# Handing out mixer steps by an account of VectorE's pending work in a hybrid retention / gated-DeltaNet step

## The chip, the cores and the metric

The kernel runs on one core of one Trainium2 chip. The metric is the device time of one execution in microseconds; a time of the kernel is the median of several runs.

## The reference

One inference step of a one-layer model with two token streams: 128 context tokens and 256 noisy latent tokens, 384 in all, of width 4096. For both:

```
mod = silu(c) @ w_ada + b_ada                  # shift, scale, gate: 3 x 4096
u   = rms_norm(h) * (1 + scale) + shift
proj = u @ w_in                                # 4096 x 16448
o_ret = retention(q, k, v), both directions    # 8 heads of 256, chunks, decay per head
o_gdn = gated_delta(conv(q), conv(k), conv(v)) # 16 heads of 128, both directions
h = h + gate * (concat(norm(o_ret)*silu(g), norm(o_gdn)*silu(z)) @ w_out)
y = rms_norm(h) * final_norm_w
```

The gated delta rule needs, for each head, direction and chunk, the inverse of a unit lower triangular matrix. The context's final states are outputs, and the latent scans start from cached states. All is float32.

## The kernel before

Every large product is done three times (high*high, high*low, low*high): a weight piece of 128x512 arrives by DMA on SP's queue, ScalarE casts it to the high part `wh` (L210), and VectorE subtracts to get the low part `wl` (L211). This is `split_tile` (L204). Pieces are prepared up to four ahead of the one that TensorE multiplies.

The work on TensorE is one long list of pieces, set when the kernel is built. First come the modulation matrices (tile `ada`) mixed with the first weight rows of many column groups. Then come 32 column groups of `w_in`, four to a pair of gated-delta heads and one retention head: group 4p gives k and q of gated-delta pair p, 4p+1 its v and z, 4p+2 and 4p+3 those of retention head p. Between them lie the pieces of the gate modulation (tile `adg`). Last come eight groups of `w_out`. When a group ends, VectorE and ScalarE take its sums out of PSUM into tiles `rawt` (`sum_done`, L540: an addition where an earlier part of the sum was kept, else copies).

When k and q of a pair or a head are there, a *mixer job* joins the list `bg_list`: `gdn(p)` (L743, 126 steps) or `ret(h)` (L1057, 33 steps). A job is a Python generator that writes a few instructions and yields. What it yields is a number of ns for the step just written, nothing (a step of `SLOT` = 1000), or a negative number: a wait for a DMA (5000 and 8000 in `gdn`). The longest VectorE steps are those of the triangular inverse, rows 2 to 31, each one multiplication (L854) and one reduction (L856), which yield 390 + 2.1 i² for row i. Before the first pair, `gates` (L671, 33 steps) prepares the decays.

The order of all instructions is a sum done at build time, with a clock of its own, here called planner ns. After each triple of large matmuls, `slot(ns)` (L186) adds 480 or 639 to the clock `now` and takes it from `next`; if `next` is at most 0, `bg_step` (L166) writes one step of the oldest job, and what `pace` (L152) returns is added to `next`. `pace` takes a base (1000 for an empty yield, else at least 500 and `PACE` times the ns; a negative yield as it is) and multiplies it by a factor f, held between `FMIN` and `FMAX`:

```
f = (due[end] - now - MARGIN) / rem
```

Here `rem` is the job's `COST` less the bases so far (for a retention head before the last, plus the cost of the next `gdn`), and no step gets less than `FLOOR` = 600. The due times come from the list of pieces: that of `gdn` p is the piece five before the end of group 4(p+1) (L1221), where the `rawt` tiles of pair p are wanted again; those of `gdn` 7 and `ret` 7 are pieces of the first `w_out` group (L1329, L1330).

If a job isn't done by then, it is drained: `new_raw` (L509) and `mix_load` (L1238) call `bg_drain`, which writes all its remaining steps in a row, with no large matmul between them. Every engine works through its instructions in the order written. Near the end, `mix_load` (POOL's queue) brings the mixers' outputs back from DRAM (`d_mix`) through two `mixl` buffers, and `mix_put` (L1246) splits them into `uh` and `ul`, the left factors of the `w_out` groups; this is written five pieces ahead of the piece that needs it.

Of the kernel before, what the change touches and what calls it, by code (L numbers as in the profile page):

```python
# [44 lines left out]
PRE = 5  # L45
RING = 5
RAW_RING = 4
PACE = 1.4
CG = 166e3
CR = 45e3  # L50
COST = {"gates": 35e3, "gdn": CG, "ret": CR}
FMIN = 0.5
FLOOR = 600.0
GATE = 1500
FMAX = 1.0
MARGIN = 1200.0
MIN_SLOT = 500.0
AHEAD = 5
# [8 lines left out]
def hybrid_step(ctx: ExitStack, tc: tile.TileContext, x_prompt, x_sample, state_ret_fwd, state_ret_bwd,  # L67
# [78 lines left out]

    urgent = []

    clock = {"next": 0.0, "now": 0.0}
    left, due = {}, {}  # L150

    def pace(tag, ns):  # L152

        base = -ns if ns and ns < 0 else (SLOT if ns is None else max(MIN_SLOT, PACE * ns))
        if tag[0] not in COST:
            return base
        left[tag] = left.get(tag, COST[tag[0]]) - base
        if ns and ns < 0:
            return base
        kind, p = tag  # L160
        rem, end = max(left[tag], base), tag
        if kind != "gdn" and p < 7:
            rem, end = rem + COST["gdn"], ("gdn", p + 1)
        return max(FLOOR, base * min(FMAX, max(FMIN, (due[end] - clock["now"] - MARGIN) / rem)))

    def bg_step():  # L166


        while urgent:
            try:  # L170
                return pace(("urgent", 0), next(urgent[0]))
            except StopIteration:
                urgent.pop(0)
        while bg_list:
            tag, job = bg_list[0]
            try:
                return pace(tag, next(job))
            except StopIteration:
                bg_list.pop(0)
        return SLOT  # L180

    def bg_drain(tag=None):
        while bg_list and (tag is None or any(t == tag for t, _ in bg_list)):
            bg_step()

    def slot(ns):  # L186
        clock["now"] += ns
        clock["next"] -= ns
        if clock["next"] <= 0:
            clock["next"] = max(clock["next"], -SLOT) + bg_step()  # L190


# [11 lines left out]
    def split_tile(raw, shape, place=None):  # L204
        if place:
            h, lo = place
        else:
            h = wpool.tile(shape, F32R, tag="wh", name="wh", bufs=RING)
            lo = wpool.tile(shape, F32R, tag="wl", name="wl", bufs=RING)
        A.copy(h, raw)  # L210
        V.tensor_tensor(lo, raw, h.bitcast(F32), op=ALU.subtract)  # L211
        return h, lo

    class Gemm:
# [15 lines left out]
        def prepare(self, i):  # L230
            if i % 2 == 0:
                self.raw = load_piece(self.src, self.chunks, self.rows(self.ks[i]), min(2, len(self.ks) - i))
            return split_tile(self.raw[:, i % 2], [128, 2, 256], self.lend and self.lend(i))

        def compute(self, i, hl):
            if self.ps is None:
                if self.ps_alloc:
                    self.ps = [self.ps_alloc(n) for n in range(3)]
                else:
                    if self.kind == "T":  # L240
                        while urgent:
                            bg_step()
                    shape, m = ([128, T], 4) if self.kind == "T" else ([128, 512], 3)
                    self.ps = [ps_main.tile(shape, F32, tag=f"mm{n}", name=f"mm{n}") for n in range(m)]
# [7 lines left out]
            for n, ps in enumerate(self.ps):  # L252
                for m, (h, lo) in self.hold:
                    k = self.ks[m]
                    st, sp = m == 0, m == end
                    if self.kind == "T":
                        wh = h[:, n // 2, (n % 2) * 128:(n % 2) * 128 + 128]
                        wl = lo[:, n // 2, (n % 2) * 128:(n % 2) * 128 + 128]
                        PE.matmul(ps, wh, high(k), start=st, stop=False)  # L259
                        PE.matmul(ps, wh, low(k), start=False, stop=False)  # L260
                        PE.matmul(ps, wl, high(k), start=False, stop=sp)  # L261
                        slot(3 * 160)
                    else:
                        a, b = high(k)[:, n * 128:n * 128 + 128], low(k)[:, n * 128:n * 128 + 128]
                        PE.matmul(ps, a, h, start=st, stop=False)  # L265
                        PE.matmul(ps, a, lo, start=False, stop=False)  # L266
                        PE.matmul(ps, b, h, start=False, stop=sp)  # L267
                        slot(3 * 213)
                if i == end:
                    self.done(n, ps)  # L270
# [4 lines left out]
    class Gates:  # L275
# [9 lines left out]
        def prepare(self, i):  # L285
            raw = load_piece(w_in, [(16384, 64)], i, 8)
            return split_tile(raw[:, :, 0], [128, 8, 64])
# [14 lines left out]
    class Ada:  # L302
# [14 lines left out]
        def compute(self, i, raw):  # L317
            if self.ps is None:
                self.ps = self.ps_alloc()
            cs = slice(256 * (i // NK), 256 * (i // NK) + 256)  # L320
            for q in range(4):
                k = i % NK + q
                PE.matmul(self.ps[32 * q:32 * q + 32, cs], cst[:, 2 * k:2 * k + 32], raw[:, q, 0],  # L323
                          start=(k < 4), stop=(k >= NK - 4), tile_position=(0, 32 * q))
            slot(450)
            if i + 4 == self.width // 256 * NK:
                self.done(self.ps)
            return 1
# [180 lines left out]
    def new_raw(owner):  # L509
        while len(live) >= RAW_LIVE:  # L510
            bg_drain(live[0])
            assert live[0] != owner
            o = live[0]
            while live and live[0] == o:
                live.pop(0)
        live.append(owner)
        return rawp.tile([128, 768], F32, tag="raw", name="rawt", bufs=RAW_LIVE)
# [22 lines left out]
    def sum_done(g, partial, last):  # L540
        kind, own, rt = groups[g][0], owner(g), rts[g // 2]

        def pre():
            if partial != "sbuf":
                kept[g] = [new_raw(own) for _ in range(2)]
            if partial == "dram":
                for i in range(2):
                    G.dma_start(out=kept[g][i], in_=d_part[g][:, 768 * i:768 * i + 768])

        def done(n, ps):  # L550
            box = kept[g]
            if kind == "T":
                t = box[n // 2][:, T * (n % 2):T * (n % 2) + T]
                if partial:
                    V.tensor_tensor(t, ps, t, op=ALU.add)  # L555
                else:
                    A.copy(t, ps)
            else:
                for i in range(2):
                    t = box[i][:, 256 * n:256 * n + 256]  # L560
                    if partial:
                        V.tensor_tensor(t, ps[:, 256 * i:256 * i + 256], t, op=ALU.add)
                    else:
                        (A.copy if i else V.tensor_copy)(t, ps[:, 256 * i:256 * i + 256])  # L564
            if last and n == (3 if kind == "T" else 2):
                for i, nm in enumerate("vz" if g % 2 else ("qk" if own[0] == "ret" else "kq")):
                    rt[nm] = box[i]
                if g % 2 == 0:
                    bg_list.append((own, gdn(own[1], rt) if own[0] == "gdn" else ret(own[1], rt)))
        return pre, done  # L570
# [822 lines left out]
```

## Time and profile before

| | |
|---|---|
| median of 3 runs | 3338.46 us (3335.72 to 3339.66) |
| profiled execution | 3342.99 us, span 3340.9 us |
| PE busy | 3256.4 us, 97% of the span |
| DVE busy | 1840.7 us, 55% |
| ACT busy | 1198.9 us, 36% |
| POOL busy | 292.2 us, 9% |

PE is TensorE, DVE is VectorE, ACT is ScalarE, POOL is GpSimd. PE's busy time counts a matmul from its start to its modelled end, and neighbours overlap, so small losses hide in it: the start-to-start distance of matmuls shows them, the idle column does not wholly. The mixers run from about 800 us to 2815 us of the span. The rows of the profile stand in the prediction.

### The profile page before, as it was taken

How to read it: one execution, taken by the hardware profiler on the slowest of the kernel's cores; microseconds unless marked ns; L12 is line 12 of the kernel's file. 1: busy time of each engine (PE TensorE's matmuls, PEld its weight loads, DVE VectorE, ACT ScalarE, POOL GpSimd, SP SyncE). 2: the span in 40 equal slices, each digit the busy share in tenths (PEclk: the TensorE clock that was granted, in tenths of full speed). 3: DMA queues.
4: the chain of work that ended last, by engine and by line, in shares of the span. 5: the costliest groups of instructions: out<-in, count | busy, mean ns of one | idle time of the engine just before them, and what ended most of it. 6: DMA issues, size and time to landing. Idle time of an engine off the chain costs nothing. (4 is left out here: it accounts for less than half of the span.)

```text
span 3340.9 us, 51824 instructions
## 1 busy us (share of the span) xinstructions
PE 3256.4 (97%) x19312; PEld 2706.2 (81%) x19312; DVE 1840.7 (55%) x3811; ACT 1198.9 (36%) x2588; POOL 292.2 (9%) x463
## 2 busy tenths in 40 slices
PE   5999999999999999999999999999999999999998
PEld 2778888877699779789789779779779877788887
DVE  2554433335855756754856746746844845444444
ACT  3322222224245235244345245235244334333333
POOL 0000000001101001001011001011000012100000
PEclk9999999999999999999999999999999999999999
DMA  9888998975534554544645645554644556645444
GB/s 304 290 287 272 330 311 266 297 251 159 179 105 135 169 153 149 179 145 140 192 146 152 185 129 156 173 154 147 177 153 141 160 153 188 187 145 170 145 151 170
DMA packets 594236, 626.14 MB, mean 187 GB/s; under 512 B 38978, under 2 KB 577042, under 8 KB 593984
## 3 DMA queue, kind: packets, MB, share of 16 engines
q1 hardware_dynamic: 570096, 551.04, 52.7%
q0 software_dynamic: 23888, 71.79, 7.3%
q8 instruction: 151, 2.47, 0.3%
q14 instruction: 101, 0.83, 0.1%
HBM read 590.37 MB, written 32.33 MB: 186 GB/s over the span
## 5 line engine op out<-in xcount | busy, mean ns | idle before, releaser
L211 DVE TENSOR_TENSOR wl<-raw,wh 128x512 fp32r<-128x512 f32 x1274 | 854.3, 687 | 939.8 <-ACT wh L210 935.8
L210 ACT CAST wh<-raw 128x512 fp32r<-128x512 f32 x1274 | 756.6, 620 | 1350.6 <-DMA raw<-in_w_in_dram 659.0
L265 PE MATMUL mm<-wh,uh 128*128 128x512 f32 x1920 | 784.3, 408 | 9.1 <-ACT rawt L564 5.6
L266 PE MATMUL mm<-wl,uh 128*128 128x512 f32 x1920 | 755.3, 393 | 6.4 <-DVE wl L211 5.8
L267 PE MATMUL mm<-wh,ul 128*128 128x512 f32 x1920 | 752.9, 392 | 0.0
L259 PE MATMUL mm<-uh,wh 128*128 128x384 f32 x2048 | 721.0, 352 | 6.2 <-DVE ul L555 3.8
L261 PE MATMUL mm<-uh,wl 128*128 128x384 f32 x2048 | 689.4, 337 | 0.0
L260 PE MATMUL mm<-ul,wh 128*128 128x384 f32 x2048 | 688.8, 336 | 0.0
L265 PEld LDWEIGHTS mm<-wh,uh 128*128 128x128 f32 x1920 | 362.2, 189 | 141.0 <-issue 48.2
L259 PEld LDWEIGHTS mm<-uh,wh 128*128 128x128 f32 x2048 | 387.3, 189 | 51.2 <-issue 34.6
L266 PEld LDWEIGHTS mm<-wl,uh 128*128 128x128 f32 x1920 | 362.7, 189 | 81.2 <-DVE wl L211 14.1
L267 PEld LDWEIGHTS mm<-wh,ul 128*128 128x128 f32 x1920 | 362.2, 189 | 78.2 <-DVE ul L1248 0.7
L260 PEld LDWEIGHTS mm<-ul,wh 128*128 128x128 f32 x2048 | 387.6, 189 | 3.9 <-issue 2.9
L261 PEld LDWEIGHTS mm<-uh,wl 128*128 128x128 f32 x2048 | 386.8, 189 | 0.0
L854 DVE TENSOR_TENSOR tmp<-M 48x4 f32<-48x4 f32 (+14 forms) x240 | 189.3, 789 | 3.4
L323 PE MATMUL ada<-adar,cst 128*32 128x256 f32 x2048 | 147.5, 404 | 26.9 <-DMA adar<-in_w_ada_dram 26.9
L645 DVE SCALAR_TENSOR_TENSOR acc<-rawt,cw,acc 128x126 f32<-128x126 f32 (+3 forms) x384 | 133.8, 413 | 12.8 <-ACT acc L640 12.8
L266 PE MATMUL o<-wl,uh 128*128 128x512 f32 x354 | 138.1, 390 | 0.2 <-DVE wl L211 0.2
L265 PE MATMUL o<-wh,uh 128*128 128x512 f32 x354 | 138.0, 390 | 0.2 <-ACT wh L210 0.2
L267 PE MATMUL o<-wh,ul 128*128 128x512 f32 x354 | 137.9, 390 | 0.0
L323 PEld LDWEIGHTS ada<-adar,cst 128*32 128x32 f32 x2048 | 53.8, 112 | 92.7 <-DMA adar<-in_w_ada_dram 42.8
L856 DVE TENSOR_REDUCE M<-tmp 48x2 f32<-48x4 f32 (+14 forms) x240 | 121.6, 507 | 8.3
(321 smaller groups left out, 2522.7 us busy)
## 6 DMA issues: line engine op xcount, KB each, us to landing
raw<-in_w_in_dram SPq DMA_DIRECT2D x1028, 256.0 KB, 3.6
adar<-in_w_ada_dram SPq DMA_DIRECT2D x256, 512.0 KB, 5.7
raw<-in_w_ada_dram SPq DMA_DIRECT2D x128, 512.0 KB, 4.3
raw<-in_w_out_dram SPq DMA_DIRECT2D x256, 256.0 KB, 3.1
rawt<-d_part POOLq DMA_DIRECT2D x26, 384.0 KB, 4.3
d_part<-spill POOLq DMA_DIRECT2D x9, 768.0 KB, 7.4
gr<-d_gc POOLq DMA_DIRECT2D x16, 384.0 KB, 7.4
d_mix<-rawt POOLq DMA_DIRECT2D x32, 192.0 KB, 2.8
```

The source lines that it names most:

```text
L210: A.copy(h, raw)
L211: V.tensor_tensor(lo, raw, h.bitcast(F32), op=ALU.subtract)
L259: PE.matmul(ps, wh, high(k), start=st, stop=False)
L260: PE.matmul(ps, wh, low(k), start=False, stop=False)
L261: PE.matmul(ps, wl, high(k), start=False, stop=sp)
L265: PE.matmul(ps, a, h, start=st, stop=False)
L266: PE.matmul(ps, a, lo, start=False, stop=False)
L267: PE.matmul(ps, b, h, start=False, stop=sp)
L323: PE.matmul(self.ps[32 * q:32 * q + 32, cs], cst[:, 2 * k:2 * k + 32], raw[:, q, 0], start=(k < 4), stop=(k >= NK - 4), tile_position=(0, ...
L645: V.scalar_tensor_tensor(out=dst[:, lo:hi], in0=x[:, lo + o:hi + o], scalar=w(t), in1=dst[:, lo:hi], op0=ALU.mult, op1=ALU.add)
L854: V.tensor_tensor(t, M[0:48, 0:i, 0:i].rearrange("p j c -> p c j"), M[0:48, i:i + 1, 0:i].to_broadcast([48, i, i]), op=ALU.mult)
L856: V.tensor_reduce(M[0:48, i, 0:i], t, axis=AX.X, op=ALU.add)
```

## The change

The planner keeps a third clock, `dve`: the time at which VectorE will have done what was given to it. Each mixer step, each weight split (`SPLIT` = 690) and each addition out of PSUM (690) is booked on it. `slot` writes no step while the account is `BACKLOG` = 1500 or more ahead of `now`. The base of a step no longer has 40% on top (`PACE` 1.0), the jobs' costs are lower, and f may rise to 2.0, so that steps may be stretched as well as shortened. No instruction is added or removed; the order in which mixer steps stand between the large matmuls changes.

```
-PACE = 1.4
-CG = 166e3
-CR = 45e3
-COST = {"gates": 35e3, "gdn": CG, "ret": CR}
+PACE = 1.0
+CG = 130e3
+CR = 28e3
+SPLIT = 690.0
+STEP = 300.0
+BACKLOG = 1500.0
+COST = {"gates": 26e3, "gdn": CG, "ret": CR}
-FMAX = 1.0
+FMAX = 2.0
...
-    clock = {"next": 0.0, "now": 0.0}
+    clock = {"next": 0.0, "now": 0.0, "dve": 0.0}
+
+    def dve(ns):
+
+        clock["dve"] = max(clock["dve"], clock["now"]) + ns
+
...
         while urgent:
             try:
-                return pace(("urgent", 0), next(urgent[0]))
+                ns = next(urgent[0])
+                dve(STEP)
+                return pace(("urgent", 0), ns)
...
             tag, job = bg_list[0]
             try:
-                return pace(tag, next(job))
+                ns = next(job)
+                dve(STEP if ns is None or ns < 0 else ns)
+                return pace(tag, ns)
...
-        if clock["next"] <= 0:
+        if clock["next"] <= 0 and clock["dve"] - clock["now"] < BACKLOG:
             clock["next"] = max(clock["next"], -SLOT) + bg_step()
...
         V.tensor_tensor(lo, raw, h.bitcast(F32), op=ALU.subtract)
+        dve(SPLIT)
         return h, lo
...
                 if partial:
                     V.tensor_tensor(t, ps, t, op=ALU.add)
+                    dve(SPLIT)
```

## The prediction

> **What bounds the kernel now.** I read the page's busy times first, then the busy times by stage, then whom TensorE waited for.
>
> ```profile
> PE 3256.4 (97%) x19312; PEld 2706.2 (81%) x19312; DVE 1840.7 (55%) x3811; ACT 1198.9 (36%) x2588; POOL 292.2 (9%) x463
> ```
>
> ```profile
> core 0: us, PE busy (x) PEld busy (x) DVE busy (x) ACT busy (x) POOL busy (x), PEclk, DMA share, GB/s
> 800.00:1000.00 200.00, 191.92 (x1172) 158.45 (x1172) 134.36 (x299) 79.43 (x185) 19.85 (x29) 0.99 0.50 150
> 1000.00:2770.00 1770.00, 1762.20 (x10419) 1486.11 (x10418) 1097.17 (x2345) 700.25 (x1595) 203.37 (x304) 1.00 0.52 157
> 2770.00:2870.00 100.00, 95.31 (x416) 76.74 (x415) 52.65 (x99) 45.38 (x92) 24.59 (x44) 0.98 0.59 175
> 2870.00:3341.00 471.00, 458.00 (x2017) 378.45 (x2015) 202.17 (x306) 155.74 (x275) 21.73 (x38) 0.99 0.51 160
> ```
>
> PE bounds it. In the mixer stages PE is idle for 8.1, 7.8 and 4.7 us, and no instruction is taken away, so all that a new order can gain is of the size of these waits. DVE has room on average (1097 of 1770 us), so only its order can hurt. The waits that end PE's idle time:
>
> ```profile
> engine line waited for: us in total, times, longest us
> PE mm L266 <- DVE wl L211: 5.8, 11, 1.8
> PE mm L265 <- ACT rawt L564: 5.6, 4, 2.3
> PE mm L265 <- ACT uh L1247: 2.8, 1, 2.8
> PE bg L1106 <- ACT qkT L1097: 1.9, 1, 1.9
> PE bg L1051 <- ACT o L1046: 1.7, 1, 1.7
> PE mm L259 <- DVE rawt L562: 1.5, 1, 1.5
> PE mm L259 <- DVE rawt L555: 0.9, 2, 0.5
> ```
>
> The first, second, sixth and seventh (13.8 us, 18 times) are large matmuls that wait for a weight split or for PSUM to be emptied. What holds these up:
>
> ```profile
> 1901.66 1.90 DVE L854 TENSOR_TENSOR tmp<-M 48x961 f32<-48x961 f32 x1
> 1903.59 1.15 DVE L856 TENSOR_REDUCE M<-tmp 48x31 f32<-48x961 f32 x1
> 1904.66 1.06 DVE L564 COPY rawt<-mm 128x256 f32<-128x256 f32 x3
> 1902.59 0.39 PE L266 MATMUL mm<-wl,uh 128*128 128x512 f32 x1
> 1905.53 0.50 PE L265 MATMUL mm<-wh,uh 128*128 128x512 f32 x1 [2.32 <-ACT rawt L564]
> ```
>
> The copies out of PSUM stand behind a row step of the triangular inverse that takes 3.05 us. From L266 to the next L265 lie 2.94 us; two matmuls at the usual 0.23 us would be 0.46. The loss is 2.48 us where the idle column has 2.32: each wait costs about 0.2 more than it shows. And it costs clock:
>
> ```profile
> 974.70:978.10 3.40, 1.74 (x10) 1.11 (x9) 0.32 (x2) 1.58 (x6) 1.35 (x1) 1.00 0.52 154
> 978.10:981.50 3.40, 3.40 (x13) 3.31 (x12) 1.58 (x3) 2.60 (x4) 0.60 (x1) 0.51 0.00 0
> 1906.50:1910.00 3.50, 3.50 (x10) 2.69 (x10) 1.90 (x3) 1.19 (x3) 1.97 (x4) 0.51 0.33 89
> 2865.70:2869.10 3.40, 3.40 (x10) 2.63 (x9) 0.83 (x2) 0.54 (x2) 2.86 (x5) 0.50 0.53 78
> 976.97 0.92 PE L1051 MATMUL bg<-ident,o 128*128 128x128 f32 x3 [1.66 <-ACT o L1046]
> 2756.25 0.78 PE L1051 MATMUL bg<-ident,o 128*128 128x128 f32 x3
> ```
>
> After the waits of 1.66, 2.32 and 2.8 us the granted clock (third number from the end) is 0.5 for 3.4 us: half of 3.4, 1.7 us, is lost each time.
>
> **The change part by part.** What moves is only the place of 1,300 steps, so I stepped the planner's sums through the list of pieces, with the old numbers and the new. One planner ns is 1.3 ns on the chip: the head transposes of pairs 0 and 7 stand at 738.5 and 2112.0 thousand planner ns and at 976.97 and 2756.25 us.
>
> Demand on DVE in planner ns: `gdn` books 64.9 thousand in named steps and 49 others at 300, 79.6 in all; its bases sum to 153.1 with `PACE` 1.4 and 128.0 with 1.0 (19.0 of it DMA waits). The weight splits book 690 for each piece of 1920, 36%. Before, a named step got 1.4 times its ns, times f: f was 0.83 for pair 0 (86% of DVE + 36% = 122%), and 1.0 for pairs 1, 2 and 4 to 7 (71 + 36 = 107%). By the new account, kept for the old order, VectorE's backlog passes 5000 in the row steps of most pairs, and has 5585 at the wait of 1902 us shown above. In the new order f is 1.0 to 1.5 in most pairs, 453 slots are held back, and outside the two drains below the backlog passes 5000 in pairs 0 and 3 alone. No emptying of PSUM falls any more beside the steps that wait for the inverse's DMA.
>
> (a) The waits for splits and PSUM: 13.8 + 18 x 0.2 + 1.7 of clock = 19.1 us is all there is. At the group ends from 800 thousand on the account has at most 3.3 thousand instead of 5.6, so I take 17. Bounds: -19.1; and -8, if half of them come back at other places.
>
> (b) The end of the `mixl` loads. PE waits 2.8 us for the last `uh` and then loses 1.7 of clock, since the last load lands late (the chain's row):
>
> ```profile
> 2859.54 4.61 DMA mixl<-d_mix
> ```
>
> The loads go through two buffers at 2.2 us each and PE takes 2.0 a piece, so PE catches up with them. In the new order `gdn` 7 and `ret` 7 run beside these loads and PE waits in (d), so the loads get ahead. Before `uh` of piece 30, PE has five pieces, 10.2 us, after (d); `d_mix`, `mixl` and the split take 0.6 + 2.8 + 3.2 + 1.1 = 7.7:
>
> ```profile
> d_mix<-rawt POOLq DMA_DIRECT2D x32, 192.0 KB, 2.8
> mixl<-d_mix POOLq DMA_DIRECT2D x32, 192.0 KB, 3.2
> ```
>
> I take the whole wait as gone: 2.8 + 0.2 + 1.7, -4.7. The other bound is 0. POOL's queue stands in order: a load written behind `gdn` 7's output DMAs waits for them, but those wait for matmuls that PE reaches at the same place, five pieces ahead of need.
>
> (c) Pair 0 comes too late. `gates` ends at 625.6 thousand (611.3 before), and pair 0 is due at 750.2. In these 124.6 thousand VectorE's account must take 79.6 for the pair and 64 splits, 44.2: 123.8, and 13 thousand of DMA waits let no step through. That doesn't fit: at the due time 21 steps are left, the tail from the first state product on, and `new_raw` writes them in a row. PE then has nothing between them:
>
> ```profile
> 1189.48 2.17 ACT L989 ACTIVATE wk<-bg,br 128x128 f32<-128x128 f32 x8 [5.27 <-PE bg L983]
> 1196.83 1.13 DVE L973 SCALAR_TENSOR_TENSOR wk<-bg,gt_neg,rawt 128x128 f32<-128x128 f32 x4 [0.20 <-PE bg L967]
> 1199.80 1.14 ACT L989 ACTIVATE wk<-bg,br 128x128 f32<-128x128 f32 x4 [3.37 <-PE bg L983]
> 1207.15 1.03 PE L1019 MATMUL bg<-S,rawt 128*128 128x256 f32 x4
> 1208.41 1.38 DVE L1031 SCALAR_TENSOR_TENSOR o<-bg,gt_eg,o 128x128 f32<-128x128 f32 x4
> 1210.78 1.35 POOL L135 TENSOR_TENSOR c<-c,half_c 128x6 f32<-128x6 f32 x1 [13.80 <-DVE c L1040]
> 1212.36 1.87 ACT L1046 ACTIVATE o<-o,c 128x128 f32<-128x128 f32 x6 [1.56 <-DVE c L1042]
> ```
>
> These rows of pair 1 give the chain. The last part is unpadded: from the end of L1019, 1208.2, to the third of six L1046, 1213.3, PE has nothing of this job: 5.1 us, and 0.9 for the second head. Before it stand 1.13 + 2.17 + 1.13 + 1.14 = 5.6 us in which PE waits if the two heads don't overlap at all. They alternate, so I take a fifth, 1.2. Idle: 7.2; bounds 5.1 and 11.6. A stretch of half clock follows, 1.7 (bounds 0 and 3.4). Gone is the wait at 976.97: 1.66 + 0.2 + 1.7 = 3.6. Sum +5.3 (bounds +1.5 and +11.4). Queued behind the drained tail on POOL is the load of `rawt` for the next group; the addition that needs it comes five pieces later, which covers it.
>
> (d) The last head comes too late. `gdn` 7 may now be stretched (f = 1.5) to its own due time: it ends at 2178 (2116 before). `ret` 7 is due at 2185.0 and has bases of 26.9 thousand: 10 of 33 steps fit, and `mix_load` writes 23 in a row.
>
> ```profile
> 2804.76 1.03 PE L1154 MATMUL bg<-rawt,kd 128*128 128x256 f32 x4
> 2799.97 0.58 ACT L1136 COPY o_r<-bg 128x512 f32<-128x512 f32 x1 [3.35 <-PE bg L1130]
> 2803.43 1.00 DVE L1140 SCALAR_TENSOR_TENSOR o_r<-bg,rq_dec,o_r 128x256 f32<-128x256 f32 x2
> 2806.35 0.89 POOL L135 TENSOR_TENSOR ssr<-ssr,half_c 128x3 f32<-128x3 f32 x1
> 2808.51 0.88 DVE L1159 SCALAR_TENSOR_TENSOR o_r<-o_r,ssr,rawt 128x256 f32<-128x256 f32 x2
> ```
>
> After the product with v: 0.58 + 2 x 1.00 + 0.8 for squares and sum + 0.89 + 1.36 = 5.6, beside two L1154 of 1.03: 3.5 us idle, 0.8 for the copies of q and k, and about 2 because the ten steps ahead (8 us of rotary products) fill DVE. Idle 6.3; with 1.7 of clock, and without the 1.9 at L1106: +6 (bounds +1.5 and +11).
>
> (e) Pair 3 is just in time with f at 0.6, as pair 0's tail was before at 0.67. I price its tail at what that one cost, +3.6 (bounds 0 and +5). Pair 5 goes down to 0.7 at its very end only: 0.
>
> (f) Outside the mixers steps move by a slot at most: 0, within 1 either way.
>
> Sum: -17 - 4.7 + 5.3 + 6 + 3.6 = -6.8 us. The profiled execution has 3342.99, 4.5 above the median; with the same step from the median, 3338.46 - 6.8 = 3331.7 us.
>
> A rule on the clock bears on (c) and (d). The rows above show half clock after waits of 1.66 to 2.8 us. The Trainium skill, TensorE: Matmul & The Clock Gate, section "What's actually happening", has the clock fall only after an idle window of about 3.4 us; these three rows speak against so long a wait. By it (d) would keep its clock and come out at +4.3, and the sum at -8.5.
>
> **The rivals.** (1) The drains decide: slower. One mechanism, the steps written in a row at the two due times, at its upper bounds: +11.4 and +11, with pair 3 at +3.6. With (a) at -8 and (b) at 0 that is +18, 3356 us. For it: they are certain in the order, and the 5.1 us gap is unpadded. Against: most of what is drained is PE's own work, and it is due anyway. It decides from drains of about 15 us together beyond what (a) brings back. (2) No change: VectorE's work is the same and a row step still takes 3.05 us, so waits come back before other matmuls; (a) brings 9, and the sum is +1: 3339 us. For it: in 1000 to 2770 us PE lost only 7.8 us in idle time. Against: the account at the group ends falls by 2000 and more. (3) A gap longer than those seen costs two stretches of half clock: (c)'s 5.1 us is such a gap, and with (d)'s, 3.4 more: 3335 us. The same page, section "HAM oscillation", says that a gap over its window throttles each time; no run here shows a gap of that length among large matmuls. (4) The change does nothing: excluded, since 453 slots are held back and two jobs drained.
>
> **How the numbers follow.** Forecast 0.48, rival 1 0.14, rival 2 0.28, rival 3 0.10. Within 0.2%, 6.7 us, a measurement can't tell this kernel from no change: 3331.8 to 3345.1. The forecast lies on that edge; two thirds of it and a little of the others fall below: faster 0.48. Rival 2 and the rest: same 0.36. Slower 0.16. The bounds of the terms add to -19.1 - 4.7 + 1.5 + 1.5 + 0 = -20.8, and to +19.4 with rival 1's and pair 3's upper bound; all terms seldom go one way, so the range is 3318 to 3350.
>
> **What would show it.** In the new profile the waits for `wl` and `rawt` should fall from 13.8 us to below 4. At about 990 us L967 to L1051 should stand in a row with one PE gap of some 5 us before L1051, and at about 2850 us L1095 to L1165 likewise; each with a stretch of clock 0.5 behind it. The wait for `uh` L1247 should be gone. I am wrong if PE idles much more than 7.2 and 6.3 us in the drained chains, if new waits for `wl` appear among the held-back steps, or if the end of the `mixl` loads still holds PE.

## The result, and the profile after

The changed kernel is slower: 3365.95 us (3361.31 to 3369.86) beside 3339.06 for the kernel before on the same chip, a ratio of 1.0077 with a 95% interval of 1.0057 to 1.0098. That is 27 us more, where 7 us less was forecast. The profiled execution took 3366.79 us, its span is 3364.8.

The table by stages, for the changed kernel (columns: us, then busy time of PE, weight loads, VectorE, ScalarE and POOL with counts, granted clock, DMA share, GB/s). The stretch from 2770 us is 30 us longer than the one shown of before, since the mixers end later:

```profile
core 0: us, PE busy (x) PEld busy (x) DVE busy (x) ACT busy (x) POOL busy (x), PEclk, DMA share, GB/s
800.00:1000.00 200.00, 188.73 (x1144) 156.97 (x1143) 132.32 (x310) 75.60 (x178) 24.02 (x35) 0.97 0.49 146
1000.00:2770.00 1770.00, 1754.08 (x10293) 1477.04 (x10292) 1086.30 (x2303) 694.51 (x1558) 197.36 (x295) 1.00 0.52 157
2770.00:2900.00 130.00, 118.83 (x576) 95.55 (x575) 71.50 (x160) 60.20 (x135) 30.73 (x53) 0.95 0.50 154
```

PE is idle for 11.3, 15.9 and 11.2 us, 38.4 in all; before it was 8.1, 7.8 and 4.7, 20.6. The second part of the loss is clock. The stretches of the mixers with a granted clock of one half, from the same view:

```profile
906.30:913.10 6.80, 5.84 (x17) 5.39 (x18) 6.73 (x11) 0.62 (x1) 0.00 (x0) 0.50 0.21 65
988.20:995.00 6.80, 4.20 (x14) 3.63 (x15) 3.00 (x8) 2.45 (x8) 3.22 (x5) 0.50 0.11 42
1834.80:1838.20 3.40, 3.40 (x10) 2.63 (x9) 3.40 (x9) 0.62 (x1) 0.00 (x0) 0.51 0.09 21
2268.20:2275.00 6.80, 5.73 (x20) 5.41 (x21) 4.02 (x7) 4.89 (x11) 0.60 (x1) 0.50 0.32 106
2858.70:2868.90 10.20, 7.29 (x19) 5.31 (x20) 4.84 (x11) 5.23 (x9) 0.63 (x2) 0.50 0.29 90
2879.20:2882.60 3.40, 3.40 (x11) 2.72 (x10) 1.71 (x3) 1.41 (x3) 1.12 (x2) 0.50 0.66 226
sum 37.40, PE 29.85 PEld 25.11 DVE 23.70 ACT 15.22 POOL 5.56; mean PE 4.98 PEld 4.18 DVE 3.95 ACT 2.54 POOL 0.93
```

PE worked 29.85 us at half speed and lost half of that, 14.9 us; before it was 10.3 us in three stretches, 5.1 lost. Idle time 17.8 more and clock 9.8 more make 27.6 us. From the first large matmul beside the mixers to the same matmul shortly behind their end, the traces have 2123.0 us before and 2150.7 after, 27.7 more. So the mixers hold the whole loss; the output projection behind that matmul takes 431.8 us in both.

Lines of the changed kernel stand 12 to 14 below those of before (`wl` L211 is L223, the head transposes L1051 are L1065). The first nine rows of PE's waits in the mixers (us in total, times, longest):

```profile
PE bg L1065 <- ACT o L1060: 10.9, 5, 4.6
PE bg L1109 <- DVE rawt L1100: 4.5, 2, 2.3
PE mm L272 <- DVE rawt L576: 3.5, 3, 1.9
PE mm L272 <- DVE rawt L568: 2.9, 1, 2.9
PE mm L279 <- DVE wl L223: 2.6, 4, 1.6
PE bg L1179 <- DVE o_r L1173: 2.3, 1, 2.3
PE bg L940 <- DVE P L934: 2.3, 2, 1.2
PE bg L1120 <- DVE qkT L1111: 2.3, 1, 2.3
PE mm L278 <- DVE rawt L568: 2.1, 1, 2.1
```

The waits for `wl` fell from 5.8 us to 2.6, as meant, and the wait for `uh` is gone. New or larger are the head transposes (five waits, before one of 1.7), `ret` 7's own products (L1109, L1120, L1179, before one of 1.9), a product inside two pairs (L940), and L568, the addition of a partial sum that is loaded back late. All waits of large matmuls for a split or for a sum out of PSUM make 12.8 us from 800 to 2900 us; before they made 12.9. So what the gate was to remove has moved, not gone.

### The profile page after: what moved, and what is told of

Its sections match the earlier page's. It is cut to its first block, busy times and chain, and to the rows that moved or that the text cites. A ratio compares the mean times of both kernels' runs of the same rounds, so it can differ in the third digit from the quotient of the medians.

```text
span 3364.8 us, 51818 instructions
## 1 busy us (share of the span) xinstructions
PE 3264.4 (97%) x19312; PEld 2709.6 (81%) x19312; DVE 1840.9 (55%) x3811; ACT 1205.4 (36%) x2588; POOL 292.9 (9%) x463
## 4 chain that ended last, share of the span: by engine, by line
PE 77%; DMA 8%; DVE 7%; issue 5%; ACT 2%; POOL 1%; SPq 1%; ACTq 0%; POOLq 0%; DVEq 0%
PE mm L278 11%; PE mm L279 10%; PE mm L280 10%; PE mm L272 9%; PE mm L274 9%; PE mm L273 9%; DMA raw<-in_w_in_dram 4%; PE o L280 3%; PE o L278 3%; PE o L279 3%; PE ada L336 2%; DVE tmp L868 2%; DVE wl L223 2%; PE adg L336 2%; DMA mixl<-d_mix 1%
## 5 line engine op out<-in xcount | busy, mean ns | idle before, releaser
L223 DVE TENSOR_TENSOR wl<-raw,wh 128x512 fp32r<-128x512 f32 x1274 | 854.1, 686 | 959.2 <-ACT wh L222 941.3
```

## The experiments

The kernels did not all run on one chip, so differences between them are taken from their ratios to the kernel before on their own chip, times 3339 us: the change costs 25.7 us by its ratio. The intervals reach 3 to 7 us to either side, so a difference between two of these ratios is uncertain by some 4 to 8 us.

**The two rows of drained steps.** The first run leaves time for `ret` 7, so that it isn't written in a row; the second lets steps through until pair 0 is due; the third does both.

```
r1, r3:  +        if kind == "gdn" and p == 7:
         +            rem, end = rem + COST["ret"], ("ret", 7)
r2, r3:  -        ... and clock["dve"] - clock["now"] < BACKLOG:
         +        ... and (clock["dve"] - clock["now"] < BACKLOG or clock["now"] < due["gdn", 0]):
```

> The changed kernel, but gated-delta pair 7 leaves room for the last retention head (its factor is taken against the due time of ret 7, with that head's cost added), so that no step of ret 7 is written in a row. Theory A (the two drains cost the time): in the changed kernel's trace the row of ret 7's steps holds about 15 us more than its matmuls, so the time falls by about 15 us, to 12 us above the kernel before. Theory B (what costs is that every job now ends only 2 to 3 thousand planner ns ahead of its due time): only the waits inside the drain fall away, but PE then meets the end of the mixl loads as it did before (2.8 us and half clock, 4.7): about 10 us less, 17 above. Theory C (the gate on VectorE's account costs the time, the drains being mostly PE's own work): within 5 us of the changed kernel.

> The changed kernel, but the gate on VectorE's account is off until pair 0's due time, so that pair 0 ends 2.2 thousand planner ns early and nothing of it is written in a row. Theory A: the 7.6 us beyond its matmuls that the row of pair 0 holds, and some of the half clock behind it, go; about 9 us less, 18 above the kernel before. Theory B: the row goes, but pair 0 still ends late with compressed steps, so half of that comes back: 4 to 5 us less. Theory C: the gate was also what held back steps in the row steps of pair 0, so the waits for weight splits from 800 to 910 us come back (about 7 us), and the sum is near zero.

> Both edits: room for ret 7 and no gate until pair 0's due time. No job is drained but for one step of pair 3. Theory A: 24 us less than the changed kernel, within 5 us of the kernel before. Theory B: 14 us less, so 10 to 15 us above the kernel before, with PE waiting for head transposes and for reloaded partial sums at the ends of the pairs. Theory C: 5 us less.

Measured: 3352.74 (ratio 1.0043, 1.0029 to 1.0057), 3354.22 (1.0048, 1.0034 to 1.0061) and 3349.34 (1.0032, 1.0019 to 1.0044). They bring 11.4, 9.7 and 15.0 us, the third as its theory B had it; the two together bring less than their sum of 21.1, though by no more than the noise. 10.7 us over the kernel before stay when no job is drained any more, but for a step of pair 3.

**Each half of the gate by itself.** r4 is the changed kernel without holding steps back; r7 is the kernel before with the account and the gate only (77 slots held, old prices and FMAX).

```
r4:  BACKLOG = 1e12
r7:  PACE, CG, CR, price of gates and FMAX as before; SPLIT = 530.0
```

> The changed kernel with the gate never closed (BACKLOG 1e12): pair 0 ends in time, ret 7 still has 21 steps written in a row. Theory A: like the run with the gate off until pair 0's due time, about 9 us less than the changed kernel. Theory B: 4 to 5 us less. Theory C: the gate is what costs, and the time falls by more than 12 us.

> The old constants (PACE 1.4, old costs, f at most 1.0) with the account and the gate alone, a weight split booked at 530: 77 slots are held back, nothing is drained. If the gate gains (theory B), 4 to 8 us faster than the kernel before, with the waits for weight splits from 800 to 910 us and for rawt at 1905 us gone or halved. If it gains nothing, within 2 us.

Measured: r4 3363.92 (1.0076, 1.0063 to 1.0089); r7 3340.91 (1.0004, 0.9995 to 1.0013). In the old order the gate neither gains nor costs. The time of r4 stayed where it was, where its three theories had it fall. Its order also has other drains than the changed kernel's, since pair 0 is in time there, so it says little alone; r16 is the clean counterpart.

**Room at the end, or no stretching.** r5 is r3 with an earlier end for each pair, r6 the changed kernel without stretching and without drains.

```
r5:  MARGIN = 12000.0
r6:  FMAX = 1.0, SPLIT = 530.0
```

> Room for ret 7, no gate until pair 0's due time, and MARGIN 12000 instead of 1200, so that every job aims to end some 12 thousand planner ns ahead of its due time (slack 7 to 13 thousand for pairs 0 to 6 instead of 1 to 3). Theory B (late ends cost: compressed tails, head transposes that wait for ScalarE, partial sums reloaded late into the rawt tiles): the waits before the head transposes (6.1 us) and for rawt behind a late reload (2.7 + 2.7 us) go with their half clock, 10 us less than with the two edits alone, so within 3 us of the kernel before. Theory A (only the drains cost, the rest is noise of the order): no change against the two edits, 10 us above the kernel before.

> The changed kernel with f held to at most 1.0 (no step is stretched) and a weight split booked at 530, its time in planner ns, so that pair 0 is not late: no job is drained, the slack is 13 to 70 thousand but for pair 0 with 1.2. The gate stays. Theory B: without stretching nothing is late but pair 0's last steps, and the gate still takes most of the waits for weight splits and PSUM (13.8 us before): 5 to 10 us faster than the kernel before. Theory C' (the gate gains nothing, waits only change their place): within 3 us of the kernel before.

Measured: r5 3356.61 (1.0047, 1.0035 to 1.0059): the waits for the late partial sum fell to 0.2 us, and waits for `wl`, for PSUM and of VectorE's split for the output products took their place, and the time is 5 above r3. Within the noise that is theory A's no change; theory B's gain of 10 did not come. r6 3358.83 (1.0053, 1.0040 to 1.0067), slower than both theories had it, with 28 waits for `wl` of 16.3 us. A shift of the whole order takes away the waits that were seen and makes others.

**Why a row of `ret` 7's steps costs 12 us.** r8 is the kernel before with its order unchanged, except that `ret` 7 stops after ten steps and the other 23 are written in a row. r10 is the same with a third buffer for the `mixl` loads, and r11 the kernel before with the third buffer.

```
r8:         if tag == ("ret", 7) and not drain: ... if held[0] > 10: return SLOT
r10, r11:  -mx.tile([128, T], F32, tag="gsb", name="mixl", bufs=2)
           +mx.tile([128, T], F32, tag="gsb", name="mixl", bufs=3)     (and "gsb" likewise)
```

> The kernel before, with one thing changed: ret 7 stops after ten steps, and its other 23 are written in a row when its output is wanted, as in the changed kernel, but with the ten rotary steps long done. If the row itself costs what the changed kernel's lost there (theory A), 10 to 13 us slower than the kernel before. If the row's chain costs what was forecast, 4.3 us idle and 1.7 of clock, and the rest came from the ten steps written right ahead of it that fill VectorE (4.5 us of waits for the rotary results), it is 2 to 5 us slower, the wait at the end of the mixl loads (4.7) being gone in exchange.

> The kernel with the old order in which 23 steps of `ret` 7 stand in a row, now with three buffers in place of two for the tiles of `mixl` (and for the gates' small tiles, which share them). Theory A (the row costs its 11 to 12 us mostly because `ret` 7's copies stand in VectorE's and ScalarE's queues behind splits of `mixl` whose loads are late for want of a buffer): the wait of 6.9 us for `qkT` at the start of the row falls to 2 to 4, the half clock behind it shrinks, and the time falls from 3352 to 3342 to 3347. Theory B (the row costs that by its own chain of dependent steps, wherever the loads are): the wait stays over 6, 3350 to 3353.

> The kernel before, with three buffers in place of two for the tiles of `mixl` and nothing else. Theory A (the loads at the end of the mixers are held up by their two buffers, and PE's 2.8 us at the last `uh`, the 1.9 us in `ret` 7 and the half clock behind them follow from it): 3332 to 3336 us, no wait for `uh` over 0.5. Theory B (the last load waits for the output of `ret` 7, not for a buffer): 3338 to 3340, the wait for `uh` as before.

Measured: r8 3351.95 (1.0036, 1.0022 to 1.0049), r10 3335.23 (0.9994, 0.9983 to 1.0006), r11 3331.79 (0.9977, 0.9967 to 0.9988). In r8 one row alone costs 12 us, and its waits from 2780 to 2900 us show where:

```profile
PE bg L1112 <- DVE qkT L1103: 6.9, 1, 6.9
PE bg L1171 <- DVE o_r L1165: 2.3, 1, 2.3
PE o L272 <- DVE wl L217: 2.0, 1, 2.0
PE mm L271 <- ACT rawt L570: 1.8, 1, 1.8
```

The longest wait is for four copies of `qkT`: two on ScalarE, 0.85 us together, and two on VectorE, 1.02 us, which end last. ScalarE's queue in front of its two (start, duration; in brackets the idle time before and what ended it):

```profile
2843.80 0.51 ACT L1253 CAST uh<-mixl 128x384 fp32r<-128x384 f32 x1 [1.16 <-DMA mixl<-d_mix]
2844.22 0.61 ACT L216 CAST wh<-raw 128x512 fp32r<-128x512 f32 x1
2845.76 0.51 ACT L1253 CAST uh<-mixl 128x384 fp32r<-128x384 f32 x1 [0.93 <-DMA mixl<-d_mix]
2846.18 0.62 ACT L216 CAST wh<-raw 128x512 fp32r<-128x512 f32 x1
2848.39 0.51 ACT L1253 CAST uh<-mixl 128x384 fp32r<-128x384 f32 x1 [1.59 <-DMA mixl<-d_mix]
2848.80 0.85 ACT L1103 COPY qkT<-bg 128x384 f32<-128x384 f32 x2
```

Every cast of a piece waits for its load, the loads land 2 to 2.6 us apart, and the copies that PE needs were written behind three of them. VectorE does the same with L1254, each time waiting for ScalarE's cast, and its two copies come behind the last of these. Both engines are idle for a good part of the time for which they hold PE up. With three buffers the same row has these waits (2750 to 2900 us of r10):

```profile
PE bg L1171 <- DVE o_r L1165: 2.3, 1, 2.3
PE o L272 <- DVE wl L217: 0.8, 1, 0.8
PE bg L1112 <- DVE qkT L1103: 0.3, 1, 0.3
```

Of 6.9 us 0.3 is left; the dependent chain's 2.3 stays whole. The time falls by 14.0 us against r8. The buffer also helps the kernel before, by 7.7 us in r11, where the waits for `uh` and in `ret` 7 are gone; so with three buffers the row costs 5.7 us (r10 against r11) where with two it costs 12, although there the wait for `uh` of the kernel before is gone in exchange. Theory A of r10 holds, and the time fell below its range: half or more of the row's price is late loads in front of it, the rest its own chain.

**The third buffer in the changed kernel**, and in the version with both edits:

> The changed kernel with three buffers in place of two for the tiles of `mixl` (and the gates' small tiles). Theory A (the row of `ret` 7 costs the changed kernel what it costs in the old order, and for the same reason): the row stays where it is, its waits fall by 5 us or more, and the time falls by 12 to 17 us, to 3349 to 3354, what giving `ret` 7 room brought. Theory B (in the changed order rotary steps still to come hold the row up, not loads): it falls by no more than 7 us, as the kernel before did, to 3359 or above.

> The changed kernel with room for `ret` 7 and the gate off until pair 0 is due (3349.3 us), now with three buffers for `mixl`. Theory A (the third buffer brings its 7 us in any order that has `mixl` loads at the end): 3341 to 3345 us. Theory B (it pays only where `ret` 7 stands among late loads): 3348 to 3350.

Measured: r12 3360.05 (1.0064, 1.0051 to 1.0078), r14 3344.19 (1.0017, 1.0008 to 1.0026). In the changed order the buffer brings 4.3 us and not 12: theory A of r12 fell. In r14 it brings 5.0, inside theory A's range. In r12 the row keeps 5.7 of the 9.1 us of waits that it has in the changed kernel (2.4 for `qkT`, 2.3 for `o_r`, 1.0 for the rotary steps). In the changed order the ten steps of decays and rotary products are written in the last 7 thousand planner ns ahead of the drained row, as the prediction had it; in r8 they had long been done. The queue of VectorE in the changed kernel, just ahead of the waiting transposes:

```profile
2850.31 0.56 DVE L1262 TENSOR_TENSOR ul<-mixl,uh 128x384 fp32r<-128x384 f32 x1 [2.79 <-ACT uh L1261]
2850.78 0.41 DVE L1079 TENSOR_SCALAR Wr<-rcon,lgam 128x384 f32<-128x384 f32 x1
...
2858.87 0.42 DVE L1100 TENSOR_TENSOR rawt<-rt 128x256 f32<-128x256 f32 x1
...
2861.78 1.02 DVE L1111 COPY qkT<-bg 128x384 f32<-128x384 f32 x2
```

First 2.79 us behind a late `mixl` piece, then 8.4 us of decay and rotary steps with splits between them and hardly a gap: both causes stand right ahead of the row.

**What is left when nothing is drained: prices, gate, margin.** r9 and r17 have the old prices and PACE, FMAX 2.0 and room for `ret` 7, without an account. r16 and r13 are the same with the prices and PACE of the change. r18 is r3 with the old prices and PACE.

```
r9:   before, FMAX = 2.0, room for ret 7                    r17:  r9 with MARGIN = 12000.0
r16:  after, BACKLOG = 1e12, room for ret 7                 r13:  r16 with MARGIN = 12000.0
r18:  r3 with PACE = 1.4, CG = 166e3, CR = 45e3, gates 35e3
```

> The kernel before with FMAX 2.0 in place of 1.0 and the one line that gives `gdn` 7 the time of `ret` 7 as well; no account of VectorE, prices and PACE as before. So the other half of the change, spreading over the time until the deadline, stands alone; no job is drained, pairs end 9 to 49 thousand planner ns ahead of their due times, where they ended 9 to 65 ahead. Theory A (spreading brings nothing by itself, since a wait that goes at one group end comes back at another place): 3336 to 3344 us, 8 to 14 us of TensorE waits on splits and PSUM, as before. Theory B (the spread order is worse than the old one, and is what is left of the loss in the two-edit version): 3346 to 3354 us, over 20 us of waits. Theory C (fewer row steps of VectorE per time help, and only the drains and the account's new prices spoil it): 3325 to 3333 us, under 6 us of waits.

> The changed kernel with room for `ret` 7, MARGIN 12000 and BACKLOG 1e12: no slot is held back and no job is drained; its prices and its PACE of 1.0 stay. Beside it stand the same kernel with the gate (299 slots held, 3356.6 us) and the old prices spread without a gate (3337.7 us). Theory A (holding slots back under the prices of the change is what costs the last 10 to 18 us: a held step is made up later in denser succession): 3335 to 3343 us. Theory B (the prices and the PACE themselves put steps at worse places): 3350 to 3358 us, over 18 us of TensorE waits.

> The changed kernel with room for `ret` 7 and BACKLOG 1e12: no slot held back, no job drained, pairs end some 2 thousand planner ns ahead of their due times. It differs from the old prices spread (3337.7 us) in PACE, CG, CR and the price of `gates` alone. Theory A (the prices and the PACE of 1.0 cost the time): 3352 to 3375 us. Theory B (the margin of 12000 made the denser order without a gate slow, not the prices): 3336 to 3345 us.

> The old prices with FMAX 2.0 and room for `ret` 7, without an account, with MARGIN 12000 in place of 1200: pairs end 18 to 25 thousand planner ns ahead of their due times where they ended 9 to 14 ahead. Theory A (the prices cost the time, an earlier end costs nothing by itself): 3336 to 3342 us. Theory B (the earlier end moves the jobs against the group ends and costs 10 us or more): 3347 to 3360 us.

> The changed kernel with room for `ret` 7 and the gate off until pair 0 is due (3349.3 us), now with the old PACE of 1.4 and the old CG, CR and price of `gates`: account, gate with SPLIT 690 (148 slots held) and spreading to the due time all stay. Theory A (the prices and the PACE are what is left of the loss): 3335 to 3342 us. Theory B (the account's gate costs the time where jobs are spread, whatever the prices): 3346 to 3352 us.

Ratios to the kernel before; no job is drained in any of these orders, but for a step of pair 3 in r3:

| | MARGIN 1200, no gate | MARGIN 12000, no gate | MARGIN 1200, gate |
|---|---|---|---|
| old prices, PACE 1.4 | 0.9996 (0.9985 to 1.0006), r9 | 0.9998 (0.9988 to 1.0007), r17 | 1.0021 (1.0013 to 1.0030), r18 |
| new prices, PACE 1.0 | 1.0055 (1.0042 to 1.0069), r16 | 1.0106 (1.0091 to 1.0122), r13 | 1.0032 (1.0019 to 1.0044), r3 |

The upper row shows that spreading to the due time costs nothing (r9, r17). Read down the first two columns: without the gate, the prices and the PACE, which were not taken apart, cost 20 and 36 us. Later ends aren't the cause, since with MARGIN 12000 the pairs end earlier and the price is higher. Read across to the third column: the gate takes back some 8 us under the new prices, and 20 where MARGIN is 12000 (r5 against r13), and costs some 8 under the old. r13's theory A, that the gate is the cost, fell, and its time lies above theory B's range as well; so did r18's, that the prices alone are: with the gate on, the intervals of old and new prices overlap (r18, r3). So in the order spreading, gate, prices, drains the change adds up from -1.3, +8.3, +3.7 and +15.0 us (r9, r18, r3, the changed kernel). The 20 us of the prices belong to another order of the same steps, in which the gate then takes some 8 of them back.

The profile shows what the prices do. Under both PACEs the job is spread to near its due time, but with 1.0 in place of 1.4 the steps that name their own ns, those with much VectorE work, are given 12% less planner time each (in `gdn` 1089 ns on average where r9 gives 1235) and the others 25% more (1246 for 993). The row steps of the inverse stand closer. PE's waits in r16, and in r9, for the same things:

```profile
PE mm L281 <- DVE wl L225: 11.0, 18, 1.3
PE mm L280 <- ACT rawt L580: 9.2, 3, 3.7
```

```profile
PE mm L267 <- ACT rawt L566: 4.6, 3, 1.8
PE mm L268 <- DVE wl L213: 4.3, 9, 1.7
```

And one of them, in the inverse of pair 5 in r16 (VectorE without an idle gap, then the matmul that waits):

```profile
2160.95 1.69 DVE L870 TENSOR_TENSOR tmp<-M 48x841 f32<-48x841 f32 x1
2162.67 1.02 DVE L872 TENSOR_REDUCE M<-tmp 48x29 f32<-48x841 f32 x1
2163.62 1.27 DVE L225 TENSOR_TENSOR wl<-raw,wh 128x512 fp32r<-128x512 f32 x2
2164.82 1.67 DVE L870 TENSOR_TENSOR tmp<-M 48x900 f32<-48x900 f32 x1
2166.52 1.08 DVE L872 TENSOR_REDUCE M<-tmp 48x30 f32<-48x900 f32 x1
2167.53 0.73 DVE L580 COPY rawt<-mm 128x256 f32<-128x256 f32 x2
2168.39 0.50 PE L280 MATMUL mm<-wh,uh 128*128 128x512 f32 x1 [3.75 <-ACT rawt L580]
```

PE stands still from 2164.64 us on. VectorE is in the middle of splits and row steps without a pause, and its copies out of PSUM come behind the next row step of 2.8 us. Adding PE's waits before large matmuls over the eight stretches in which a pair's inverse runs (each from its first row step to 5 us past its last) gives 8.8 us before, 8.0 in r9, 7.5 in r17, 17.5 in r16 and 23.8 in r13; with the gate 7.2 in the changed kernel, 7.0 in r3 and 6.1 in r18. Over all the mixers PE is idle for 35.2 us in r16 and 20.7 in r9, and half clock costs 11.4 and 5.1, 20.8 us together, which is the whole of what the prices cost without the gate. So the gate does just what it is built for: it takes the extra 10 us out of these stretches, which the change's own prices put in. It can't take out much of the 8.8 that were there before, and the steps that it holds back come later.

**The version that the runs point to**: r15 is r9 with three buffers.

> The old prices with FMAX 2.0 and room for `ret` 7 (no account), with three buffers for `mixl`: the version that the runs point to. Theory A (spreading moves nothing and the buffer brings 7 us): 3329 to 3334 us, as the kernel before with three buffers. Theory B (with the loads early, fewer row steps per time pay as well): 3322 to 3328.

Measured: 3334.58 (0.9987, 0.9977 to 0.9997). It beats both kernels, but isn't below r11 (0.9977): the one edit of a buffer in the kernel before has the lowest ratio of all that ran, and spreading adds nothing to it that the noise lets one see.

## Why the prediction was wrong, point by point

- **What bounds the kernel**: right. PE does; the loss is waits and the clock behind them, in the mixers alone.
- **(a), the step that failed.** It took the account in planner ns for the time at which PE waits, and credited 17 of 19.1 us, with the waits to fall from 13.8 us (0.9 of them ahead of the mixers) to below 4. They went from 12.9 to 12.8. Waits for `wl` did fall, but beside the inverse's rows all waits of large matmuls went only from 8.8 to 7.2 us, and 5.0 us at L568 are new. Alone in the old order the gate brings nothing (r7: 1.0004). The account doesn't hold the time in which VectorE stands idle for ScalarE's cast, for a DMA or for PE; r8's rows show PE waiting for engines that are idle. Nor is all of VectorE's work on it: of the sums out of PSUM it books the additions of the gated-delta groups, not each one. The additions and copies of the retention groups (L576, L578, 22.7 us of VectorE from 780 to 2900 us) and the splits of `mixl` (L1262, 17.6 us) are left out, and no run books them, so what that would change isn't known.
- **The prices, a term that wasn't in the sum.** The prediction worked out that f is 1.0 to 1.5 and that the bases sum to 128 instead of 153 thousand, and put no price on it. Without the gate they cost 20 us (r16 against r9), the largest single effect found at MARGIN 1200; with the gate on, 3.7 (r3 against r18), no more than the noise.
- **(b)**: right on the wait, which is gone, but not on the reason: r1 and r3, in which no row of `ret` 7 holds PE up, have no wait for `uh` either. r11 has 7.7 us for an earlier landing of these loads, where 4.7 was forecast for the end alone.
- **(c)**: idle 7.2 forecast. PE's idle time from 800 to 1000 us is 11.3 us (8.1 before), with a wait of 4.6 before the head transposes:

```profile
990.80 0.48 PE L1065 MATMUL bg<-ident,o 128*128 128x128 f32 x1 [4.59 <-ACT o L1060]
```

  The row itself has this wait and one of 0.7 us, 5.3 where 7.2 was forecast, and the clock behind it (6.8 us at half speed, 4.2 of them busy) loses 2.1 for 1.7. Less the 3.4 that stood there before (idle 1.7, clock 1.7), that is +4.0; +5.3 was forecast, bounds 1.5 and 11.4. Letting pair 0 be in time brings 3.7 us (r3 against r1, within the noise) to 9.7 (r2 against the changed kernel).
- **(d), mis-sized.** Forecast +6 with an upper bound of 11; taking the row away brings 11.4 (r1), and putting it into the old order costs 12 (r8). The sentence "the loads get ahead" was the wrong way round: the loads stand in front of the row in both engines' queues. By terms: the rotary steps were 4.5 us for 2, the copies of q and k 2.3 for 0.8, the chain's end 2.3 for 3.5, so 9.1 of idle time for 6.3; and the clock was half for 13.6 us, 10.7 of them busy, so 5.3 lost for 1.7. Less the 1.9 at L1106 that stood there before, that is 12.5, which agrees with r1 within its noise.
- **(e)**: the size came out by luck. Pair 3's end has 1.1 us before its head transposes, and 2.9 for a wait that the prediction had ruled out in (c): five pieces were to cover the load of `rawt`. Behind pair 0 no such load stands in the trace; the first beside the mixers is issued at 1266 us. At pair 3, whose job ends at its due time, POOL issues the load behind that job's last transfers and the next head's loads, and the addition waits for it:

```profile
1767.06 0.54 POOL L1068 DMA_DIRECT2D d_mix<-rawt  x1 [0.52 <-PE mm L274]
1769.74 0.73 POOL L1075 DMA_DIRECT2D Sr<-in_state_ret_fwd_dram  x1 [2.13 <-ACT wh L222]
1771.20 1.11 POOL L561 DMA_DIRECT2D rawt<-d_part  x2
1777.40 1.66 DVE L568 TENSOR_TENSOR rawt<-mm,rawt 128x384 f32<-128x384 f32 x3 [3.34 <-DMA rawt<-d_part]
1778.11 0.41 PE L272 MATMUL mm<-uh,wh 128*128 128x384 f32 x1 [2.94 <-DVE rawt L568]
```

- **(f)**: right, 0 for the output projection. Ahead of the mixers the changed kernel's trace is 3.7 us shorter, but traces of one order differ by more there: the mixers' first product starts at 769.2 us in the kernel before, 769.0 in r8, 762.0 in r10 and 763.3 in r11.
- **The rivals.** Rival 1 (the drains decide, 3356 us) has the right direction, and drains are 15 us of the 26; rival 2 (waits come back elsewhere) is right too: L568's 5.0 us and the 6.3 of the head transposes outside pair 0 are such waits. Each was priced as if the other weren't there, and neither had the prices in it. Rival 3 is right in part: with the wait of 4.59 us before the head transposes of pair 0 the clock is down for 6.8 us, two stretches, and so it is at 2268 us with a wait of 3.85 before those of pair 5. But in r1 a wait of 4.58 us at pair 0 has one stretch only (988.8 to 992.2 us), so the length of the wait alone does not settle it.
- **The clock rule.** The Trainium skill, TensorE: Matmul & The Clock Gate, section "What's actually happening", lets the clock fall only after some 3.4 us of idling. This trace disagrees again: in `ret` 7's row no wait is over 2.33 us, and 10.2 us at half speed lie there. The forecast of (d) at +4.3 by that rule would have been further off.
- **The sum and the range.** From the two traces, idle time and lost clock: the waits of (a) +2.8 (idle -0.1, clock 2.9) where -17 was forecast, (b) -4.5, (c) +4.0, (d) +12.5, and 13.5 for the rest, where (e) had 3.6: the head transposes of four pairs (6.3, and 2.9 of clock at pair 5) and products inside the pairs (L940, L964, L997 at 2807 us, 4.3). Less 1.1 us of small waits that went, that is 27. The bounds of the terms added to 3358; the range stopped at 3350, on the ground that all terms seldom go one way, and here (a) and (d) both went beyond their upper bounds.

What stays open is why the gate costs 8 us where jobs with the old prices are spread (r18 against r9), while it costs nothing where they aren't (r7). The traces show other waits (6.2 us for PSUM, 4.3 us of one output product for its split in r18), but no common cause.

## What to carry to other kernels

An in-order engine can hold others up while it is idle: before a step is written ahead of another, look at what the operations in front of it wait for, not only how long they work. A planner that books work alone can't see that; here one more buffer for a late load (r11, 7.7 us; r10, 14.0 us against r8) did more for the kernel before than any order that was tried. When a change alters several constants of a planner at once, price each: the gate, spreading and the margin looked guilty or useful by turns, and the table of six versions showed that the new prices make waits, which the gate then removes in part.

## What was not expected of the hardware

Waits of PE of 2.1 to 2.3 us in close succession were followed by a half clock for up to 10.2 us, three of the 3.4 us stretches seen before, and the six stretches of the changed kernel cost 14.9 us beside 38.4 us of idle time, where before they cost 5.1 beside 20.6. So the waits of the changed kernel cost about 40% more than PE's idle time says, those of the kernel before 25%. A stretch of half clock doesn't come with every such wait, however: before the head transposes of pair 0, PE waits 1.7 us in the kernel before and in r8, r10 and r11 alike, and the granted clock from 970 to 985 us is 0.89 in the first and 1.00 in the other three. So a difference of one stretch, 1.7 us, between two traces need not come from the edit.
